# A decoder layer on one core: a shared vector loaded wide, column sums formed in steps, and a tail without filler products

## The chip, the cores and the metric

One Trainium2 chip, one of its cores. The metric is the device time of one execution in microseconds (us), the median of several runs. TensorE, VectorE, ScalarE, GpSimd and SyncE each work through their own list of instructions in order, and wait for each other by semaphores. SyncE issues all loads and stores here. In the profile TensorE is PE (its weight loads are PEld), VectorE DVE, ScalarE ACT, GpSimd POOL, SyncE SP or SPq.

## What is computed

One layer on 256 tokens of 2048 channels, in float32. Cut to what matters:

```
h   = x @ w_in                                  # gMLP u, v; attention q, k, v; two gates
mix = (sigmoid(ga) * (ya @ w_out_a) + sigmoid(gb) * (ob @ w_out_b)) @ w_o
x   = layer_norm(ALPHA * x + mix, ln1_g, ln1_b)
idx, w = route(x, router_w, router_bias)        # top 2 of 16 experts inside one group
ffn = moe(x, idx, w, w_gate, w_up, w_down)      # silu(x Wg) * (x Wu) @ Wd, weighted
ple = sigmoid(x @ ple_w_gate) * (p @ ple_w_proj)
x   = layer_norm(ALPHA * x + ffn + ple, ln2_g, ln2_b)
```

## The kernel before

Nearly all loads are weights: tiles of 128 x 4096 float32, 2 MB each, in the order in which they are used (list `loads`). They go into a pool of twelve large buffers (`B`), where the kernel's long-lived arrays lie too. `done` gives a tile's buffer free once its products are issued, and `prefetch` issues the next load then. SyncE's list is thus: weight, weight, ..., with the small loads where the program asks for them. A load also waits for an earlier load: eight semaphores serve all loads in turn (DMAHW0 to DMAHW7 in the rows of the order).

Short-lived arrays of 128 x 512 come from a pool of five slots (`S`): a new one waits until every reader of the slot's last array has finished.

The first half of the program (projections, attention, output projection) splits each weight piece of 512 columns in two: ScalarE copies it rounded (L267), VectorE takes the difference (L268), three pieces ahead of TensorE, which multiplies both (L286). Four buffers `pc` hold the pieces. Small work that has no place of its own stands in a queue `bg`; one item is taken after every second piece, so a block of 16 pieces takes eight items. The output projection has four blocks (loop `for i in range(4)`), each followed by VectorE's two residual adds (L531) and two statistics (L523). The router's products run on rows that are not normalised yet, and for that the column sums of the router's weights, scaled by ln1_g and ln1_b, are needed: `column_sums` (L513) forms them by two products, two reductions (L516, L517), a product with ones (L519) and a copy (L520), as one item of `bg` in the fourth block.

The expert stage goes over eight pairs of experts (`for g in range(NP)`). For a pair: gate and up products in two halves "A" and "B" (`inner`, L815, eight weight tiles each), then the down products "0" and "1" (`outer`, L822, four tiles each). `evac` (L880, L881) splits the result in yh (ScalarE) and yl (VectorE), `scatter` (L893) puts the rows back by two products, the second of them with yl, and VectorE adds (L898). The scatters of "0" run between the products of "1". A gated embedding `ple` (L793, L798; GpSimd adds it, L805) follows some stages. In the last pair the down products come in narrowing columns (`last_columns`), so that little is left after the last load.

In the pair before the last, ahead of that `evac` of "0", the second norm's vectors are brought in: `gb2` holds ln2_g for columns 0 to 1535 on all partitions, ln2_g and ln2_b for the last 512 columns on all partitions, and in two rows both vectors for columns 0 to 1535. For each vector there is one row load (L1050), one load of 2 KB into a slot `ends` (L1052) and GpSimd's broadcast of it (L1053); a third broadcast (L1054) spreads columns 0 to 1535.

At the end, the last 512 columns are normalised by VectorE alone; for the others a product of two rows (L1095) gives what is added, six times, each followed by VectorE (L1098) and a store. Between these six, `busy(1)` (L547) issues a product of ones with ones.

Of the kernel before, what the change touches and what calls it, by code (L numbers as in the profile page):

```python
# [13 lines left out]
OP = mybir.AluOpType  # L14
AX = mybir.AxisListType
# [4 lines left out]
DC = 16  # L20
NH = 8
NE = 16
# [14 lines left out]
def trunk(ctx, tc, I, out):  # L37
# [19 lines left out]
    def S(name, dt=F32):  # L57
        return tp.tile([128, 512], dt, name=name, tag="t")
# [100 lines left out]
    bg = deque()  # L159
# [350 lines left out]
    lrs = C("lrs", [128, 2])  # L510
    lnm = C("lnm", [128, 2])

    def column_sums():  # L513
        rwb = S("rwb").rearrange("p (c e) -> p c e", c=DC)
        for k, t in ((0, rwg), (1, rwb)):
            DVE.tensor_tensor(t, rw, gc[:, k, :, None].to_broadcast([128, DC, 32]), op=OP.mult)  # L516
            DVE.tensor_reduce(red[:, k], t.rearrange("p c e -> p e c")[:, 0:NE, :], axis=AX.X, op=OP.add)  # L517
        ps = AUX()
        PE.matmul(ps[:, 0:2 * NE], ones, red.rearrange("p k e -> p (k e)"), start=True, stop=True)  # L519
        DVE.tensor_copy(rsb.rearrange("p k e -> p (k e)"), ps[:, 0:2 * NE])  # L520

    def stats(i, a):
        DVE.bn_stats(lst[:, a, i, :], x1[:, a, i * 512:(i + 1) * 512])  # L523

    for i in range(4):
        if i == 3:
            bg.extend([None, column_sums])
        ps = block(mixh, mixl)
        for a in range(2):
            xb = x1[:, a, i * 512:(i + 1) * 512]  # L530
            DVE.scalar_tensor_tensor(xb, xb, ALPHA, ps[a], op0=OP.mult, op1=OP.add)  # L531
            if i < 3:
                stats(i, a)
# [470 lines left out]
    for g in range(NP):  # L1004
        xg, i = xgs[g % 2], g % 2
        following = []
        if g < NP - 1:
            P = Pm[:, 1 - i]
            following.append(lambda P=P, g=g: onehot(P, pair_of(pos, g + 1)))
            if g == 0:  # L1010
                following.extend([lambda P=P, cp=cp: gather(P, xgs[1], cp) for cp in range(8)])
            else:
                following.extend(gathers(P, xgs[1 - i]))
            following.append(lambda P=P, g=g, i=i: selection(P, pair_of(wA, g + 1), 1 - i, g + 1))
        if g == 1:
            bg.extend([None, lambda: keep(2), None, None, None, None])
            bg.extend([lambda q=q, a=a: split_x1(q, a) for q in range(4) for a in range(2)])
        if g > 0:
            bg.extend(following)
        if g == 1:  # L1020
            bg.extend([keep, None, None] + [lambda pr=pr: keep_T(pr) for pr in range(8)] + [free])
        if g == 2:
            bg.extend([lambda q=q, a=a: residual(q, a) for q in range(4) for a in range(2)])
        if g == OVER - 1:
            bg.extend([None] * 20 + [keep])
        if g == NP - 2:
            bg.append(lambda: (free(2), keep()))
        if g == OVER:
            for f in back:
                f()  # L1030
            back = []
            keep(-1)
            overflow()
        ps = inner("A", g, xg, events(back, 1))
        s = hidden(ps, g)
        ples(g, "A")
        ps = inner("B", g, xg, {3: lambda: turn_hidden(s, hTs[0]), **({11: keep} if g == 0 else {})})
        s = hidden(ps, g)
        ples(g, "B")
        if g == 0:  # L1040
            take_late()
            bg.extend(following)
        ps = outer("0", g, {2: lambda: turn_hidden(s, hTs[1]), **({3: keep} if g == 0 else {})})
        if g == 0:
            long["acc"] = BR("acc").rearrange("p (a d) -> p a d", a=2)
        if g == NP - 2:
            gb2 = BR("gb2")
            gbr = gb2[0:2, 2560:4096]
            for k, r in enumerate((I["ln2_g"], I["ln2_b"])):
                SP.dma_start(gb2[k:k + 1, 2560:4096], r[:, 0:1536])  # L1050
                ends = S("ends")
                SP.dma_start(ends[0:1, :], r[:, 1536:2048])  # L1052
                POOL.partition_broadcast(gb2[:, 1536 + 512 * k:2048 + 512 * k], ends[0:1, :], channels=128)  # L1053
            POOL.partition_broadcast(gb2[:, 0:1536], gb2[0:1, 2560:4096], channels=128)  # L1054
        y = evac(ps)
        ples(g, "0")
        at = events(scatters(y, i, 0, g == 0, 0 if g == NP - 1 else None), 1)
        if g == NP - 1:
            last_columns(g, at)
            break  # L1060
        ps = outer("1", g, at)
        drain()
        back = scatters(evac(ps), i, 1024, g == 0)
        ples(g, "1")
# [28 lines left out]
    for n, (q, a) in enumerate((q, a) for q in range(3) for a in range(2)):  # L1093
        ps = MM()
        PE.matmul(ps, rowc[:, a * 128:(a + 1) * 128], gbr[:, q * 512:(q + 1) * 512], start=True, stop=True)  # L1095
        if n < 5:
            busy(1)
        DVE.scalar_tensor_tensor(part(q, a), part(q, a), rstd[:, a:a + 1], ps, op0=OP.mult, op1=OP.add)  # L1098
        store(q, a)

# [63 lines left out]
```

## Time and profile before

| what | value |
|---|---|
| median of three runs | 1624.52 us (1622.77 to 1625.68) |
| the profiled execution | 1626.4 us, its span 1624.7 us |
| mean granted clock of TensorE in it | 0.984 |
| busy: PE, DVE, ACT, POOL | 97%, 34%, 25%, 2% of the span |
| loads and stores | 540.07 MB, 332 GB/s over the span |
| the chain that ended last | PE 26%, DMA 5% of the span |

Busy time counts an instruction from start to modelled end, so a matmul that waits in a full pipeline is busy too. The granted clock is a share of 2.4 GHz; 0.50 is 1.2 GHz. Idle time in brackets stands in front of the instruction, with what ended it. A wait for several things is put down to the one that came last.

### The profile page before, as it was taken

To read this page: it belongs to the slowest core of one execution; us is meant where nothing else is said; L and a number is where in the kernel's file an instruction comes from. 1 tells how busy PE (TensorE), PEld (TensorE's weight loads), DVE (VectorE), ACT (ScalarE), POOL (GpSimd) and SP (SyncE) were. 2 spreads that over 40 slices of the span, in tenths; PEclk is the share of its full clock that TensorE was granted. 3 is DMA by queue.
4 is the path that set the end of the run, shared out by engine and by line. 5 is a ranking of instruction groups with operands and counts; after the bars stand their busy time and mean duration, and the time that the engine had idled before them with its cause. 6 is when DMAs were issued, how large, how long until landed. Compare 5 with 4: busy or idle time off the path is not lost. (4 is left out here: it accounts for less than half of the span.)

```text
span 1624.7 us, 17427 instructions
## 1 busy us (share of the span) xinstructions
PE 1575.2 (97%) x7191; PEld 910.7 (56%) x7191; DVE 548.2 (34%) x948; ACT 407.9 (25%) x717; POOL 37.9 (2%) x43
## 2 busy tenths in 40 slices
PE   8999999999999999999999999999999999985998
PEld 6888878888888875343335353433535353522433
DVE  6555575556556653022222112021011112001105
ACT  5455555454554432011111001001000101000000
POOL 0000000000000000000000000000000000000002
PEclk9999999999999999999999999999999999996998
DMA  9843454354556848999999999998999999999893
GB/s 388 336 156 123 182 201 164 148 184 180 207 186 261 333 159 339 423 426 427 428 427 427 369 426 428 426 427 372 429 426 428 426 428 428 427 428 394 348 428 156
DMA packets 43613, 540.07 MB, mean 332 GB/s; under 512 B 7172, under 2 KB 7172, under 8 KB 10760
## 3 DMA queue, kind: packets, MB, share of 16 engines
q1 hardware_dynamic: 43528, 538.90, 80.8%
q8 instruction: 58, 0.95, 0.2%
q14 instruction: 27, 0.22, 0.0%
HBM read 536.78 MB, written 2.10 MB: 332 GB/s over the span
## 5 line engine op out<-in xcount | busy, mean ns | idle before, releaser
L286 PE MATMUL mm<-pc,xh 128*128 128x512 f32 x1152 | 362.9, 395 | 5.8 <-ACT pc L267 5.2
L268 DVE TENSOR_TENSOR pc<-w,pc 128x512 fp32r<-128x512 f32 x416 | 290.8, 709 | 200.9 <-ACT pc L267 198.2
L267 ACT ACTIVATE pc<-w 128x512 fp32r<-128x512 f32 x416 | 259.6, 630 | 238.0 <-DVE pc L268 179.0
L286 PEld LDWEIGHTS mm<-pc,xh 128*128 128x128 f32 x1152 | 214.0, 189 | 50.9 <-ACT pc L267 5.7
L815 PE MATMUL mm<-w,xg 128*64 128x512 f32 x1024 | 235.3, 604 | 6.1 <-PEq L953 6.1
L822 PE MATMUL mm<-w,hT 128*64 128x512 f32 (+2 forms) x1088 | 236.8, 577 | 3.5 <-DMA w<-in_exp_w_dram 3.5
L815 PE MATMUL mm<-w,late 128*64 128x512 f32 x1024 | 231.0, 597 | 0.0
L286 PE MATMUL mm<-pc,xl 128*128 128x512 f32 x576 | 225.5, 391 | 0.0
L822 PEld LDWEIGHTS mm<-w,hT 128*64 128x64 f32 x1088 | 72.5, 137 | 131.7 <-issue 124.9
L815 PEld LDWEIGHTS mm<-w,xg 128*64 128x64 f32 x1024 | 69.4, 138 | 135.1 <-issue 127.1
L815 PEld LDWEIGHTS mm<-w,late 128*64 128x64 f32 x1024 | 69.0, 136 | 131.0 <-issue 130.4
L286 PEld LDWEIGHTS mm<-pc,xl 128*128 128x128 f32 x576 | 108.5, 188 | 23.1
L798 PE MATMUL mm<-w,x1T 128*128 128x256 f32 x512 | 112.0, 379 | 0.0
L798 PEld LDWEIGHTS mm<-w,x1T 128*128 128x128 f32 x512 | 97.2, 190 | 13.2
L286 PE MATMUL mm<-pc,mixh 128*128 128x512 f32 x256 | 80.2, 394 | 0.0
L859 DVE TENSOR_TENSOR s<-s,mm 128x256 f32<-128x256 f32 x32 | 13.4, 418 | 194.5 <-ACT s L858 194.5
L858 ACT ACTIVATE s<-mm 128x256 f32<-128x256 f32 x32 | 12.3, 383 | 224.3 <-PE mm L815 214.9
L898 DVE TENSOR_TENSOR acc<-acc,aux 128x512 f32<-128x512 f32 (+2 forms) x60 | 38.6, 650 | 87.2 <-PE aux L893 85.3
L880 ACT ACTIVATE yh<-mm 128x512 fp32r<-128x512 f32 (+1 forms) x32 | 18.5, 590 | 185.1 <-PE mm L822 185.1
L881 DVE TENSOR_TENSOR yl<-mm,yh 128x512 fp32r<-128x512 f32 (+1 forms) x32 | 21.6, 682 | 113.2 <-ACT yh L880 78.9
L286 PEld LDWEIGHTS mm<-pc,mixh 128*128 128x128 f32 x256 | 48.6, 191 | 10.1
L286 PE MATMUL mm<-pc,mixl 128*128 128x512 f32 x128 | 50.3, 393 | 0.0
(215 smaller groups left out, 929.4 us busy)
## 6 DMA issues: line engine op xcount, KB each, us to landing
w<-in_exp_w_dram SPq DMA_DIRECT2D x184, 2048.0 KB, 17.9
w<-in_w_in_dram SPq DMA_DIRECT2D x34, 2048.0 KB, 8.7
w<-in_w_o_dram SPq DMA_DIRECT2D x8, 2048.0 KB, 8.3
w<-in_ple_w_gate_dram SPq DMA_DIRECT2D x8, 2048.0 KB, 20.3
w<-in_exp_d_last_dram SPq DMA_DIRECT2D x7, 2048.0 KB, 27.9
w<-in_w_out_a_dram SPq DMA_DIRECT2D x4, 2048.0 KB, 8.2
w<-in_w_out_b_dram SPq DMA_DIRECT2D x4, 2048.0 KB, 8.1
w<-in_w_in_dram SPq DMA_DIRECT2D x3, 1024.0 KB, 10.3
```

Of the source, the lines that this page charges most:

```text
L267: ACT.activation(hi, w, AF.Copy)
L268: DVE.tensor_sub(lo, w, hi.bitcast(F32))
L286: PE.matmul(ps[a], l[:, c, as_], r, start=(first and n == 0), stop=(last and n == 2))
L798: PE.matmul(ps[:, a * 256:(a + 1) * 256], x1T[:, c, a * 128:(a + 1) * 128], w[:, c, :], start=(c == 0 and a == 0), stop=(c == DC - 1), ski ...
L815: PE.matmul(ps[k][es, :], x[:, es], w[:, e, k, :], start=(c == 0), stop=(c == DC - 1), skip_group_check=True, tile_position=(0, 64 * e))
L822: PE.matmul(p[es, 0:n], hTs[fc // 4][:, fc % 4, es], w[:, e, b * n:(b + 1) * n], start=(fc == 0), stop=(fc == 7), skip_group_check=True, t ...
L858: ACT.activation(s[:, ks], pg[:, ks], AF.Sigmoid)
L859: DVE.tensor_mul(s[:, ks], s[:, ks], pg[:, ks])
L880: ACT.activation(h, p[:, 0:n], AF.Copy)
L881: DVE.tensor_sub(l, p[:, 0:n], h.bitcast(F32))
L898: DVE.tensor_add(xb, xb, ps[:, 0:n])
```

## The change

Three edits.

- The last 512 columns of ln2_g and ln2_b are loaded by one load each straight to all 128 partitions of `gb2` (256 KB instead of 2 KB). The slots `ends` and their two broadcasts are gone.
- The column sums are no longer one item of `bg`. From the third block on, each product and each reduction is an item, then come three empty items, then the product with ones and its copy. The slot `rwb` is taken ahead of the loop.
- The products of ones between the six two-row products are gone.

```
+    rwb = S("rwb").rearrange("p (c e) -> p c e", c=DC)
+
     def column_sums():
-        rwb = S("rwb").rearrange("p (c e) -> p c e", c=DC)
-        for k, t in ((0, rwg), (1, rwb)):
-            DVE.tensor_tensor(t, rw, gc[:, k, :, None].to_broadcast([128, DC, 32]), op=OP.mult)
-            DVE.tensor_reduce(red[:, k], t.rearrange("p c e -> p e c")[:, 0:NE, :], axis=AX.X, op=OP.add)
         ps = AUX()
         PE.matmul(ps[:, 0:2 * NE], ones, red.rearrange("p k e -> p (k e)"), start=True, stop=True)
         DVE.tensor_copy(rsb.rearrange("p k e -> p (k e)"), ps[:, 0:2 * NE])
 
+    def sums_bg():
+        for k, t in ((0, rwg), (1, rwb)):
+            bg.append(lambda k=k, t=t: DVE.tensor_tensor(t, rw, gc[:, k, :, None].to_broadcast([128, DC, 32]),
+                                                         op=OP.mult))
+            bg.append(lambda k=k, t=t: DVE.tensor_reduce(red[:, k], t.rearrange("p c e -> p e c")[:, 0:NE, :],
+                                                         axis=AX.X, op=OP.add))
+        bg.extend([None, None, None, column_sums])
...
     for i in range(4):
-        if i == 3:
-            bg.extend([None, column_sums])
+        if i == 2:
+            sums_bg()
         ps = block(mixh, mixl)
...
             for k, r in enumerate((I["ln2_g"], I["ln2_b"])):
                 SP.dma_start(gb2[k:k + 1, 2560:4096], r[:, 0:1536])
-                ends = S("ends")
-                SP.dma_start(ends[0:1, :], r[:, 1536:2048])
-                POOL.partition_broadcast(gb2[:, 1536 + 512 * k:2048 + 512 * k], ends[0:1, :], channels=128)
+                SP.dma_start(gb2[:, 1536 + 512 * k:2048 + 512 * k], r[:, 1536:2048].to_broadcast([128, 512]))
             POOL.partition_broadcast(gb2[:, 0:1536], gb2[0:1, 2560:4096], channels=128)
...
         PE.matmul(ps, rowc[:, a * 128:(a + 1) * 128], gbr[:, q * 512:(q + 1) * 512], start=True, stop=True)
-        if n < 5:
-            busy(1)
         DVE.scalar_tensor_tensor(part(q, a), part(q, a), rstd[:, a:a + 1], ps, op0=OP.mult, op1=OP.add)
```

How instructions stand on the engines, at three places. VectorE in the third and fourth blocks of the output projection, before (L268 is a split, `x16` sixteen in a row, L531 and L523 are residual adds and statistics at a block's end):

```order
L268 TENSOR_TENSOR pc<-w,pc 128x512 x16
L531 SCALAR_TENSOR_TENSOR x_3540<-x_3540,mm 128x512
L523 BN_STATS lst<-x_3540 128x6
L531 SCALAR_TENSOR_TENSOR x_3540<-x_3540,mm 128x512
L523 BN_STATS lst<-x_3540 128x6
L268 TENSOR_TENSOR pc<-w,pc 128x512 x4
L516 TENSOR_TENSOR rwg<-rw,gc 128x512
L517 TENSOR_REDUCE red<-rwg 128x16
L516 TENSOR_TENSOR rwb<-rw,gc 128x512
L517 TENSOR_REDUCE red<-rwb 128x16
L520 COPY rsb<-aux 128x32
L268 TENSOR_TENSOR pc<-w,pc 128x512 x9
```

And now (line numbers of the changed kernel: L537 and L529 are the adds and statistics):

```order
L268 TENSOR_TENSOR pc<-w,pc 128x512 x2
L522 TENSOR_TENSOR rwg<-rw,gc 128x512
L268 TENSOR_TENSOR pc<-w,pc 128x512 x2
L524 TENSOR_REDUCE red<-rwg 128x16
L268 TENSOR_TENSOR pc<-w,pc 128x512 x2
L522 TENSOR_TENSOR rwb<-rw,gc 128x512
L268 TENSOR_TENSOR pc<-w,pc 128x512 x2
L524 TENSOR_REDUCE red<-rwb 128x16
L268 TENSOR_TENSOR pc<-w,pc 128x512 x8
L518 COPY rsb<-aux 128x32
L537 SCALAR_TENSOR_TENSOR x_3540<-x_3540,mm 128x512
L529 BN_STATS lst<-x_3540 128x6
```

The four operations stood in one run between splits of the fourth block; now two splits lie between any two of them, one block earlier, and the copy stands at that block's end.

VectorE at the end of "0" of the pair before the last, with what each instruction waits for, before (L859 and L860 form the hidden values, L870 copies them turned):

```order
L860 SCALAR_TENSOR_TENSOR s<-s,wc,mm 128x256 [waits DVE_49]
L870 COPY hT_4297<-aux 128x256 [waits Activation_49]
L881 TENSOR_TENSOR yl<-mm,yh 128x512 [waits Activation_49]
L881 TENSOR_TENSOR yl<-mm,yh 128x512 [waits DMAHW3_49,Activation_49,Pool_49]
L898 TENSOR_TENSOR acc<-acc,aux 128x512 [waits PE_49] x4
L881 TENSOR_TENSOR yl<-mm,yh 128x512 [waits DVE_49,Activation_49] x2
```

And now:

```order
L866 SCALAR_TENSOR_TENSOR s<-s,wc,mm 128x256 [waits DVE_49]
L876 COPY hT_4297<-aux 128x256 [waits Activation_49]
L887 TENSOR_TENSOR yl<-mm,yh 128x512 [waits Activation_49] x2
L904 TENSOR_TENSOR acc<-acc,aux 128x512 [waits PE_49] x4
L887 TENSOR_TENSOR yl<-mm,yh 128x512 [waits DVE_49,Activation_49]
L887 TENSOR_TENSOR yl<-mm,yh 128x512 [waits DVE_49,Activation_49,Pool_49]
```

The second split of the first two waited for a load and for GpSimd, now for neither; the last split of the next two ("1" of that pair) now names GpSimd.

SyncE around the same place, before (w are weights of the last pair, each behind one of the eight semaphores):

```order
L137 DMA w<-in_exp_w_dram 128x4096 [waits DMAHW1_49,PE_49]
L1050 DMA gb_7941<-in_ln_g_dram 1x1536 [waits DMAHW2_49,PE_49]
L1052 DMA ends<-in_ln_g_dram 1x512 [waits DVE_49,DMAHW3_49,Activation_49,Pool_49]
L1050 DMA gb_7941<-in_ln_b_dram 1x1536 [waits DMAHW4_49]
L1052 DMA ends<-in_ln_b_dram 1x512 [waits DMAHW5_49,DVE_49,Pool_49]
L137 DMA w<-in_exp_w_dram 128x4096 [waits DMAHW6_49,PE_49]
```

And now:

```order
L137 DMA w<-in_exp_w_dram 128x4096 [waits DMAHW1_49,PE_49]
L1056 DMA gb_7941<-in_ln_g_dram 1x1536 [waits DMAHW2_49,PE_49]
L1057 DMA gb_7941<-in_ln_g_dram 128x512 [waits DMAHW3_49]
L1056 DMA gb_7941<-in_ln_b_dram 1x1536 [waits DMAHW4_49]
L1057 DMA gb_7941<-in_ln_b_dram 128x512 [waits DMAHW5_49]
L137 DMA w<-in_exp_w_dram 128x4096 [waits DMAHW6_49,PE_49]
```

Four loads stand in the same four places; two of them are wide and wait for no engine.

## Rows read from the trace of the kernel before

**Rows 1.** The page's span in 40 slices: TensorE and DMA busy, in tenths.
```profile
PE   8999999999999999999999999999999999985998
...
DMA  9843454354556848999999999998999999999893
```

**Rows 2.** Stretches of the tail: us; PE, PEld, DVE, ACT, POOL busy; clock, DMA share, GB/s.
```profile
1440.00:1457.00 17.00, 14.04 (x62) 4.53 (x58) 0.69 (x1) 1.19 (x2) 0.00 (x0) 1.00 1.01 427
1458.00:1482.00 24.00, 0.00 (x0) 0.00 (x0) 0.62 (x2) 0.00 (x0) 1.46 (x3) 0.55 1.01 427
...
1488.00:1512.00 24.00, 24.00 (x112) 16.06 (x108) 2.48 (x4) 1.79 (x3) 1.27 (x1) 1.00 0.61 233
1512.00:1592.00 80.00, 80.00 (x362) 26.54 (x362) 13.94 (x24) 3.47 (x8) 4.51 (x4) 1.00 1.01 428
1592.00:1596.00 4.00, 4.00 (x32) 2.23 (x30) 1.72 (x3) 0.60 (x1) 0.59 (x1) 1.00 0.55 227
```

**Rows 3.** Timeline around TensorE's long wait: start us, us, engine, line, operation [idle before].
```profile
1447.96 3.65 PE L822 MATMUL mm<-w,hT 128*64 128x512 f32 x16 [1.23 <-DMA w<-in_exp_w_dram]
...
1457.70 0.22 SPq L1052 DMA_DIRECT2D ends<-in_ln_g_dram  x1
...
1480.54 1.48 POOL L1053 PARTITION_BROADCAST gb<-ends  x2 [76.13 <-DMA w<-in_exp_w_dram]
1481.38 0.69 DVE L881 TENSOR_TENSOR yl<-mm,yh 128x512 fp32r<-128x512 f32 x1 [34.09 <-POOL gb L1053]
1481.88 1.80 POOL L1054 PARTITION_BROADCAST gb<-gb  x1
...
1482.12 0.80 PE L893 MATMUL aux<-yl,PO 128*128 128x512 f32 x1 [24.46 <-DVE yl L881]
...
1482.85 3.68 PE L822 MATMUL mm<-w,hT 128*64 128x512 f32 x8
...
1494.85 13.98 PE L798 MATMUL mm<-w,x1T 128*128 128x256 f32 x64
```

**Rows 4.** Timeline of VectorE in the output projection's last blocks.
```profile
563.86 0.68 DVE L531 SCALAR_TENSOR_TENSOR x<-x,mm 128x512 f32<-128x512 f32 x1
...
583.65 0.69 DVE L268 TENSOR_TENSOR pc<-w,pc 128x512 fp32r<-128x512 f32 x1 [0.67 <-ACT pc L267]
...
585.62 0.68 DVE L531 SCALAR_TENSOR_TENSOR x<-x,mm 128x512 f32<-128x512 f32 x1
...
591.05 0.69 DVE L516 TENSOR_TENSOR rwg<-rw,gc 128x512 f32<-128x512 f32 x1
591.77 0.58 DVE L517 TENSOR_REDUCE red<-rwg 128x16 f32<-128x256 f32 x1
...
611.41 1.38 DVE L531 SCALAR_TENSOR_TENSOR x<-x,mm 128x512 f32<-128x512 f32 x2 [3.40 <-PE mm L286]
```

**Rows 5.** Timeline of TensorE at the product with ones of the column sums.
```profile
593.71 0.61 PE L519 MATMUL aux<-red,hT 128*128 128x32 f32 x2 [2.61 <-DVE red L517]
594.13 1.20 PE L286 MATMUL mm<-pc,mixh 128*128 128x512 f32 x2
```

**Rows 6.** Timeline of TensorE in the last columns and at the six two-row products (L1095).
```profile
1589.72 4.52 PE L822 MATMUL mm<-w,hT 128*64 128x512 f32 x28
...
1598.73 1.97 PE L822 MATMUL mm<-w,hT 128*64 128x128 f32 x32
...
1607.90 1.12 PE L1095 MATMUL mm<-gb,late 2*128 2x512 f32 x2 [0.46 <-ACT late L1089]
...
1610.64 2.00 PE L1095 MATMUL mm<-gb,late 2*128 2x512 f32 x2
...
1618.20 2.07 PE L1095 MATMUL mm<-gb,late 2*128 2x512 f32 x2
```

**Rows 7.** DMA issues, 150 to 250 us: KB each, us from issue to landing.
```profile
ug<-in_gmlp_ln_b_dram SPq DMA_DIRECT2D x1, 512.0 KB, 7.6
```

**Rows 8.** A stretch among the two-row products, columns as in rows 2.
```profile
1612.00:1616.00 4.00, 4.00 (x6) 1.05 (x6) 1.50 (x2) 0.00 (x0) 0.00 (x0) 0.50 0.34 131
```

## The prediction

> **What bounds the kernel now.** I read the page's slices first, then the tail by stretches, then the instructions around the one long hole in TensorE, then the two smaller places that the change touches.
>
> In the slices TensorE is busy at 0.9 nearly throughout and the DMA engines are full in most slices of the second half [rows 1]. So in the expert stage two resources are near their limits at once, and what a hole costs depends on which one is ahead. The stretches of the tail say it [rows 2]. From 1440 to 1457 us the DMA engines move 427 GB/s and TensorE is busy 14.04 of 17 us: weights are late. The reader sees it at single tiles: the products of a weight tile start 1.23 us after TensorE had nothing left, when the load lands, and take 3.65 us [rows 3]. From 1458 to 1482 TensorE does nothing at all, the loads go on at 427 GB/s, and the granted clock drops (0.55, that is mostly 1.2 GHz). From 1488 to 1512 the picture is turned: TensorE is busy 24 of 24 us and the loads fall to 233 GB/s, because the buffers that filled in the hole are not free. From 1512 to 1592 both are full, and the loads end between 1592 and 1596.
>
> The hole itself [rows 3]: TensorE starts the second product of a scatter at 1482.12, after 24.46 us of waiting for VectorE's split yl. VectorE waits 34.09 us for GpSimd's broadcast out of "ends". GpSimd waits for the four small loads; SyncE issues the first of "ends" at 1457.70, behind weights already asked for, and the broadcasts start at 1480.54. So yl stands only because its slot in the five-slot pool was lent to "ends".
>
> **Edit 1: the wide load.** It removes "ends", thus the wait (the order rows of the split show it without the GpSimd and DMA waits), and two broadcasts of about 0.74 us each on GpSimd, which lie on no path once yl is free. What is late next? Not TensorE's own work but the weights, as before 1457. TensorE alone would gain 24.46 us and some 3 us of slow clock (eight products took 3.68 us at 1482.85 instead of 1.9 at full clock [rows 3]). The weights allow less: the bytes of the tail stay, and only the time in which the loads ran below rate can come back. That is the stretch of 24 us at 233 GB/s against 428: 24 x (1 - 233/428) = **10.9 us**. For this the buffers must never fill. The longest product group that holds them is the 14 us of L798 [rows 3], in which 14/4.9 = 3 tiles arrive (4.9 us a tile: 2 MB at 428 GB/s); in the 24 us of the hole five tiles arrived and the loads had not slowed yet, so there is room.
>
> The wide loads add bytes: 256 KB each. At the stream's 428 GB/s each takes 0.6 us. A bound from above is the 512 KB broadcast of the first norm's vectors, two together landing 7.6 us after issue [rows 7], so at most 3.8 us for our two; a load that stands first in a full queue does not pay the issue latency, so I take 0.6 us each, 1.2 us in all, ends 1.2 and 3.8. All four loads now stand before the next weight tile in SyncE's queue as the four small ones did, with the same lane waits; GpSimd's remaining broadcast (1.8 us) and the gated-embedding add behind it wait until they land, near 1482, and the add's input comes only after L798 of that pair, near 1485 (the end of its row in rows 3 less the hole), so nobody waits.
>
> Last, TensorE trailed the loads at the end: the third-last tile's products began near 1592.3 (12 of the 28 in the row at 1589.72 belong to the tile before) [rows 6], some 1.2 us after its load can have landed (1596 less 4.9 for the 2 MB behind it). On the heels of the loads it trails by some 0.3 us: **1 us** more, bounds 0 and 4 (the last tile's products begin halfway through the row at 1598.73, near 1599.7, the loads end by 1596). After that the chain is TensorE's own and unchanged. Edit 1: 10.9 - 1.2 + 1.0 = 10.7 us, bounds 7.1 and 13.7.
>
> **Edit 2: column sums in steps.** Blocks of the output projection are 21.76 us apart (563.86 to 585.62, first residual add to first residual add); the one that holds the sums takes 25.79 us (to 611.41) [rows 4]: 4.03 us more. The reason is in the rows: four VectorE operations in one go from 591.05 on (0.69 and 0.58 us, twice), while TensorE waits 2.61 us for the reduction, and the products after it run at half clock (two took 1.20 us) [rows 5]. Now each of the four stands alone between two pairs of splits. VectorE's cycle there is 0.69 us busy and 0.67 idle [rows 4]; a pair of pieces has 1.34 us idle, an added operation takes 0.69 or 0.58. So they hide. At the head of that block VectorE is still paying the two adds and two statistics of the block before (0.68 us each); the first added operation comes two splits later. If that cover is gone, TensorE stands up to 0.69 us per operation and the gain goes. The product with ones moves to the block's end, where its input is long ready; it keeps 0.2 us of TensorE (0.4 at half clock [rows 5]). The copy of its result waits for it with VectorE's residual adds queued behind, and those wait for the same last products. Gain 4.03 - 0.2 = 3.8 us, bounds 0 and 4.0. TensorE is the only busy resource from there to 1093 us and the loads are paced by the buffers it frees, so I carry it in full; 0 is the other bound.
>
> **Edit 3: no ones between two-row products.** From 1607.90 to 1620.27 six two-row products and five of ones run in a row, 12.4 us [rows 6]. The ones did not hold the clock: in the stretch from 1612 TensorE is busy 4.00 of 4 us at 0.50 [rows 8]. The first product starts at 1607.90, follows to the next in 1.05 us at full clock, and the third runs slow already (the clock falls about 2.8 us in). If it falls there again, 2.7 products go at 1.05 and 3.3 at 2.0: 9.5 us, gain **2.9**. If it falls at once: 12.0, gain 0.4; if never: 6.3, gain 6.1. I take 2.9, since the fall came with the ones in place. VectorE's add (0.75 us) and the stores hide behind the next product.
>
> By the Trainium skill (TensorE: Matmul & The Clock Gate, Part 1) a busy engine is held at 2.4 GHz and an idle one at 1.2; by that alone all six would stay fast and edit 3 would give 6.1. The row at 0.50 with TensorE fully busy speaks against it for two-row products.
>
> **Sum.** 10.7 + 3.8 + 2.9 = 17.4 us. The profiled execution took 1626.4 us (span 1624.7), so 1609.0 in its place; it stands 1.9 above the median of the runs, 1624.5, and on that scale I forecast **1607.1 us**.
>
> **The rivals.**
> *Column sums give nothing at the end* (10%): VectorE falls behind as said, or the weights absorb it. For: the loads bind before 1457. Against: below rate at 1488 and before, they follow TensorE's frees. Time 1624.5 - 13.6 = 1610.9.
> *The clock holds in the last six* (6%): gain 6.1 instead of 2.9, 1603.9. Against: rows 8.
> *Edit 1 does not do what it says* (5%): another reader holds yl's slot, or the second pair of splits inherits the GpSimd wait that the order rows show there. For: that wait is printed. Against: GpSimd's only other reader of that pool is the embedding add of long before. Then 1624.5 - 6.7 = 1617.8.
> *Slower* (3%): with the hole gone TensorE waits for weights at every tile to the end, and its clock could fall there. At half clock a tile takes 7.3 us (twice 3.65; eight took 3.68 [rows 3]) against 4.9 for its load, 2.4 us each; of some 24 tiles left it is slower by over 0.2% from 20.6/2.4, nine, on; with twelve, 1636. Against: from 1440 to 1457, with just such waits, the granted clock is 1.00 [rows 2].
> The same page (section on HAM oscillation) reports a thin-product kernel that fell back to the slow clock at every weight tile it waited for; by that all tiles would be slow, and the case would be the likeliest. The stretch at 1.00 disagrees, so I leave it at 3%.
>
> **How the numbers follow.** The forecast has 76%, the rivals 10, 6, 5 and 3. A measurement of this kernel tells about 0.2%, 3.2 us, from no change. All but the last case are faster by more; of its 3% one part ends within. Faster 0.97, same 0.01, slower 0.02. The range: downwards the clock case and 4 us of lag, 1602.5; upwards the column case with dear wide loads, 1612.5. It leaves out the stall that stays, the slower case and the tails of the first.
>
> **What would show it.** Right: no wait of yl on GpSimd and no standing of TensorE over 3 us after 1400; loads above 420 GB/s until they end, near 1582 (1595 less 9.7 less 3.8); TensorE waiting about 1.2 us at weight tiles at clock 1.00 in the last 80 us; blocks of the projection all near 21.8 to 22.0 us; the six two-row products in 9 to 10 us. Wrong: loads that still fall below rate after 1480, a projection block above 23 us, or a clock of 0.50 before the last columns.

## The result, and the profile after

The changed kernel takes 1607.47 us (median of four runs, 1606.60 to 1610.06); the kernel before, on the same chip, 1625.10 (1622.77 to 1626.67). The ratio is 0.9895, with a 95% interval of 0.9878 to 0.9912: 17.6 us less. The forecast was 1607.1 in a range of 1602.5 to 1612.5. The profiled execution took 1607.34 us, its span 1605.6, so 19.1 us less span than before.

The slices of the page, to be held against [rows 1], with the rate of the loads:

```profile
PE   8999999999999999999999999998999999999978
...
DMA  9843453445556858999999999999999999999995
GB/s 388 345 158 112 182 204 146 183 158 209 176 191 262 326 201 319 418 427 427 428 426 428 365 428 427 427 426 377 429 427 427 427 427 427 427 429 422 428 427 204
```

The slices with 8 and 5 near the end of TensorE's line are gone, and so is the dip in the loads behind them. The same stretches as in [rows 2], and the end of the loads (us; busy times; clock, DMA share, GB/s):

```profile
1440.00:1457.00 17.00, 15.28 (x64) 4.68 (x60) 4.14 (x6) 1.19 (x2) 0.00 (x0) 1.00 1.00 426
1458.00:1482.00 24.00, 21.99 (x94) 16.08 (x92) 2.07 (x3) 1.79 (x3) 1.80 (x1) 0.93 1.00 420
1482.00:1512.00 30.00, 30.00 (x135) 9.74 (x133) 3.73 (x7) 0.77 (x2) 1.26 (x1) 1.00 1.01 428
1512.00:1570.00 58.00, 46.07 (x207) 14.63 (x204) 4.68 (x10) 2.70 (x6) 0.00 (x0) 1.00 1.01 427
...
1578.00:1580.00 2.00, 2.00 (x19) 1.03 (x15) 0.69 (x1) 0.60 (x1) 0.40 (x1) 1.00 0.62 254
1580.00:1582.00 2.00, 2.00 (x14) 1.28 (x14) 1.23 (x2) 0.00 (x0) 0.00 (x0) 1.00 0.35 147
1582.00:1584.00 2.00, 2.00 (x27) 1.53 (x24) 1.86 (x4) 0.38 (x1) 1.73 (x2) 1.00 0.00 0
```

In the tail the loads no longer fall to 233 GB/s before they end; they are over at 1582, where before they still ran at 227 from 1592 to 1596 [rows 2]. What bounds the tail now can be read in the fourth row: TensorE stands 12 us in the 58 up to 1570, at a clock of 1.00. It waits for weights. Timeline of TensorE (start us, us, engine, line, operation, idle before):

```profile
1442.67 3.65 PE L828 MATMUL mm<-w,hT 128*64 128x512 f32 x16 [1.24 <-DMA w<-in_exp_w_dram]
...
1462.96 3.02 PE L799 MATMUL aux<-late 128*128 128x256 f32 x8 [2.01 <-DMA late<-in_ple_w_proj_dram]
...
1567.97 1.94 PE L828 MATMUL mm<-w,hT 128*64 128x512 f32 x8 [1.24 <-DMA w<-in_exp_d_last_dram]
...
1575.52 4.52 PE L828 MATMUL mm<-w,hT 128*64 128x512 f32 x28
```

Where the hole of 24.46 us stood [rows 3], the longest wait is 2.01 us, for a small load of the gated embedding, which the hole had covered. The 28 products of the last columns start 14.20 us earlier than in [rows 6]. VectorE's split yl (line 887 now) waits no more for GpSimd. The view of that tile gives the instruction (ns shortest/median/longest), and what VectorE waited for ahead of it (us, times):

```profile
L887 DVE TENSOR_TENSOR yl<-mm,yh x32: 425/692/693, 709.5 to 1583.5; 128x512 fp32r<-128x512 f32 x31, 128x256 fp32r<-128x256 f32 x1
its engine sat idle before it (us, times) until:
  ACT yh L886: 81.7, 26
  DVE yl L887: 0.4, 1
```

VectorE in the projection's last two blocks, to be held against [rows 4]:

```profile
563.64 0.68 DVE L537 SCALAR_TENSOR_TENSOR x<-x,mm 128x512 f32<-128x512 f32 x1
...
567.47 0.69 DVE L522 TENSOR_TENSOR rwg<-rw,gc 128x512 f32<-128x512 f32 x1
569.28 0.62 DVE L524 TENSOR_REDUCE red<-rwg 128x16 f32<-128x256 f32 x1
...
585.74 0.68 DVE L537 SCALAR_TENSOR_TENSOR x<-x,mm 128x512 f32<-128x512 f32 x1
...
606.83 1.38 DVE L537 SCALAR_TENSOR_TENSOR x<-x,mm 128x512 f32<-128x512 f32 x2 [3.40 <-PE mm L286]
```

The block with the four operations takes 22.10 us and the last one 21.09, where before it was 21.76 and 25.79. Last, the six two-row products, one row now, VectorE's last adds, which wait for them, and the stretches in which they run:

```profile
1593.70 7.53 PE L1099 MATMUL mm<-gb,late 2*128 2x512 f32 x12 [0.46 <-ACT late L1093]
...
1599.56 0.75 DVE L1100 SCALAR_TENSOR_TENSOR acc<-acc,frs,mm 128x512 f32<-128x512 f32 x1 [0.96 <-PE mm L1099]
1601.27 0.75 DVE L1100 SCALAR_TENSOR_TENSOR acc<-acc,frs,mm 128x512 f32<-128x512 f32 x1 [0.96 <-PE mm L1099]
```

```profile
1594.00:1596.00 2.00, 2.00 (x6) 0.79 (x5) 1.03 (x2) 0.00 (x0) 0.00 (x0) 1.00 0.64 228
1596.00:1597.00 1.00, 1.00 (x4) 0.51 (x3) 0.89 (x2) 0.00 (x0) 0.00 (x0) 0.92 0.53 207
1597.00:1601.00 4.00, 4.00 (x5) 1.09 (x4) 1.81 (x3) 0.00 (x0) 0.00 (x0) 0.50 0.62 210
```

The six products take 7.53 us, 12.37 before [rows 6]; the clock falls just before 1597 and stays at 0.50 with TensorE busy all the time, as in [rows 8].

So the 19.1 us of the two traces split at three places. Up to the fourth block's residual adds it is 4.6 us (611.41 and 606.83; 0.2 of it lay there before the third block). From there to the row of 28 products it is 9.6 (978.31 and 968.69 us long), and in the last six products 4.8.

### The profile page after: what moved, and what is told of

The parts are those of the page before. It is cut to its first block, busy times and chain, and to the rows that moved or that the text cites. A ratio compares the mean times of both kernels' runs of the same rounds, so it can differ in the third digit from the quotient of the medians.

```text
span 1605.6 us, 17410 instructions
## 1 busy us (share of the span) xinstructions
PE 1568.4 (98%) x7186; PEld 909.0 (57%) x7186; DVE 548.5 (34%) x948; ACT 408.0 (25%) x717; POOL 36.6 (2%) x41
## 5 line engine op out<-in xcount | busy, mean ns | idle before, releaser
L268 DVE TENSOR_TENSOR pc<-w,pc 128x512 fp32r<-128x512 f32 x416 | 290.9, 710 | 197.2 <-ACT pc L267 194.4
```

The source lines that it names most:

```text
L268: DVE.tensor_sub(lo, w, hi.bitcast(F32))
```

## The experiments

The kernels of one set ran on the same chip and share the runs of the kernel before; there are three sets, named in the headings. Three lengths are read off each trace and shown together further down: the third and fourth projection blocks, the way from there to the 28 products, and the last six products.

### Each edit alone (first set)

**Edit 1 alone.** On the kernel before:

```
-                ends = S("ends")
-                SP.dma_start(ends[0:1, :], r[:, 1536:2048])
-                POOL.partition_broadcast(gb2[:, 1536 + 512 * k:2048 + 512 * k], ends[0:1, :], channels=128)
+                SP.dma_start(gb2[:, 1536 + 512 * k:2048 + 512 * k], r[:, 1536:2048].to_broadcast([128, 512]))
```

> The kernel before with edit 1 alone. Theory (the slot lent to `ends` held yl, and behind it only weights are late): no wait of yl on GpSimd, no standing of TensorE over 3 us after 1400 us, loads at some 428 GB/s to their end. The prediction's sum gives 10.7 us less than before (7.1 to 13.7); what the changed kernel's trace leaves when about 4.4 us is taken for edit 2 (two projection blocks 4.36 us shorter) is 14.2 - 4.4 = 9.8 us less. Rival 1, TensorE's own time set the end: the whole hole comes back, 24 us or more less. Rival 2, edit 1 works only together with edit 2: 2 us less or nothing.

Measured: 1617.37 us against 1625.11, ratio 0.9950 (0.9937 to 0.9964): 7.7 us less, interval 5.9 to 10.2. In the trace the way from the projection to the 28 products is 968.79 us, 9.5 less than before. VectorE's yl waits for ScalarE and for itself only (81.9 and 0.4 us in all), TensorE's longest wait after 1400 us is 2.0 us, and the loads run at 424 to 428 GB/s in the stretches from 1458 to 1570. So the tail's gain is edit 1's and needs no help from edit 2, and both rivals fall: 24 us do not come back, and neither is it nothing. The median lies below the 9.8 that the theory gave, inside the interval.

**Edit 2 alone.** On the kernel before, the first two pieces of the change's diff: the operations as items of `bg` from the third block on.

> The kernel before with edit 2 alone. Theory (a block of the projection some 4 us shorter, TensorE the only busy resource there, so all of it is carried to the end): 3.8 to 4.4 us less than before. Rival, weights absorb it, since the hole at 1458 us waits for loads and stays where it is: 0 to 1 us less, with the hole longer by what the blocks gain.

Measured: 1622.01 us, ratio 0.9980 (0.9971 to 0.9989): 3.1 us less, interval 1.8 to 4.7. The hole is still there, and as long as it was but for 0.2 us ([rows 3] has 24.46):

```profile
1477.90 0.79 PE L899 MATMUL aux<-yl,PO 128*128 128x512 f32 x1 [24.68 <-DVE yl L887]
```

It moved 4.2 us to the front (from 1482.12). The weights did not absorb the gain.

**Edit 3 alone.** On the kernel before:

```
         PE.matmul(ps, rowc[:, a * 128:(a + 1) * 128], gbr[:, q * 512:(q + 1) * 512], start=True, stop=True)
-        if n < 5:
-            busy(1)
```

> The kernel before with edit 3 alone. Theory after the changed kernel's trace (two-row products in a row take 0.86 us each at full clock and 1.71 at half, and not the 1.05 and 2.0 that stood between products of ones): 4.8 us less than before. The prediction's own pricing: 2.9 us less. If the clock falls at once: 0.4 less; if it never falls: 6.1 less.

Measured: 1621.92 us, ratio 0.9981 (0.9971 to 0.9991): 3.2 us less, interval 1.5 to 4.7. The trace gives more, 7.50 us where there were 12.37:

```profile
1607.28 7.50 PE L1095 MATMUL mm<-gb,late 2*128 2x512 f32 x12 [0.46 <-ACT late L1089]
```

Of the four prices written down this trace fits 4.8, while the median lies nearest to 2.9; its interval shuts out 0.4 and 6.1, and 4.8 lies just outside it. The three medians add up to 14.0 us, the whole change has 17.6. With intervals of 3 to 4 us each that is no contradiction, and the lengths in the traces add up.

**The slot alone.** On the kernel before: the narrow load and the broadcast stay, but in the vector's own place.

```
-                ends = S("ends")
-                SP.dma_start(ends[0:1, :], r[:, 1536:2048])
-                POOL.partition_broadcast(gb2[:, 1536 + 512 * k:2048 + 512 * k], ends[0:1, :], channels=128)
+                own = gb2[0:1, 1536 + 512 * k:2048 + 512 * k]
+                SP.dma_start(own, r[:, 1536:2048])
+                POOL.partition_broadcast(gb2[:, 1536 + 512 * k:2048 + 512 * k], own, channels=128)
```

> The kernel before, with the 2 KB load put into row 0 of its final place and GpSimd's broadcast done in place: no slot is lent, but the narrow load and both broadcasts stay. Theory (the lent slot alone made the hole; the wide load is only another way to do without it, and costs its bytes): 10.7 + 1.2 = 11.9 us less than before, so 0.5 to 3.8 us less than the run with the wide load. Rival, GpSimd's broadcasts or their wait for the small loads cost time in themselves: the hole or a part of it stays, at most 5 us less than before.

Measured: 1615.21 us, ratio 0.9932 (0.9918 to 0.9947): 9.9 us less, interval 8.6 to 13.3, and 2.2 less than with the wide load. GpSimd waits as long as ever for the small loads and broadcasts as late as before ([rows 3]: 1480.54), and nobody stands for it:

```profile
1480.53 1.48 POOL L1053 PARTITION_BROADCAST gb<-gb  x2 [76.01 <-DMA gb<-in_ln_b_dram]
1481.87 1.80 POOL L1054 PARTITION_BROADCAST gb<-gb  x1
```

So it was the lent slot and not the broadcast that made the hole. The wide load looks like the dearer way to do without the slot, by 2.2 us at the medians, whose ranges do not overlap (1616.25 to 1617.56 and 1612.42 to 1615.55).

### What the wide load costs (second and third set)

**Each wide load twice.** On the changed kernel:

```
+                for _ in range(2):
-                SP.dma_start(gb2[:, 1536 + 512 * k:2048 + 512 * k], r[:, 1536:2048].to_broadcast([128, 512]))
+                    SP.dma_start(gb2[:, 1536 + 512 * k:2048 + 512 * k], r[:, 1536:2048].to_broadcast([128, 512]))
```

> The changed kernel with each wide load issued twice, so 0.52 MB more. The run with the narrow load in its own row was about 2.1 us faster than the one with the wide load, where the prediction had priced the two wide loads at 1.2. Theory (a wide load costs more than its bytes at the stream's rate): 2 us or a little more over the changed kernel, about 1609.6 us. Rival, bytes alone: 1.2 us more, 1608.7. Rival, hidden: 1607.5, and the 2.1 us then come from elsewhere.

Measured: 1617.77 us, 10 more than the changed kernel's 1607.47: none of the three. The way to the 28 products, 978.64 us, is as long as it was with the hole. The experiment measured something else. The second load writes where the first one does and so waits for its landing, and SyncE stands with all the weights behind it. Its timeline (the time of a row reaches from the first issue to the last), and the stretches there:

```profile
1453.07 26.12 SPq L1058 DMA_DIRECT2D gb<-in_ln_g_dram  x2
1479.24 0.28 SPq L1056 DMA_DIRECT2D gb<-in_ln_b_dram  x1
1479.58 4.70 SPq L1058 DMA_DIRECT2D gb<-in_ln_b_dram  x2
1484.38 15.60 SPq L137 DMA_DIRECT2D w<-in_exp_w_dram  x10
```

```profile
1453.00:1479.00 26.00, 23.73 (x99) 15.58 (x98) 2.76 (x4) 1.19 (x2) 1.80 (x1) 0.93 0.89 375
1479.00:1485.00 6.00, 6.00 (x28) 2.88 (x26) 0.69 (x1) 0.60 (x1) 0.20 (x1) 1.00 0.44 90
```

From 1453 to 1484 us no weight is asked for, and the DMA engines run dry (share 0.44 at the end of it). Against 428 GB/s the two stretches lose 3.2 and 4.7 us of load time; the bytes of 0.52 MB are 1.2 us. So most of the 10 us is the price of a load that waits for a landing in the queue that all weights share.

**Two wide loads more, into other columns.** On the changed kernel; GpSimd's last broadcast writes over them.

```
                 SP.dma_start(gb2[:, 1536 + 512 * k:2048 + 512 * k], r[:, 1536:2048].to_broadcast([128, 512]))
+                SP.dma_start(gb2[:, 512 * k:512 + 512 * k], r[:, 1536:2048].to_broadcast([128, 512]))
```

> The changed kernel with two wide loads more (256 KB each), into columns that GpSimd's last broadcast writes over afterwards, so that no load waits for another's landing, as it did in the run with each load issued twice. Theory (about 1 us a wide load): 2 us more than the changed kernel. Rival, bytes at the stream's rate: 1.2 us more. Rival, hidden: no difference. If it is 5 us or more, it is not the bytes but the places that small loads take in SyncE's queue in front of the weights.

**The changed kernel again**, in the same set:

> The changed kernel once more, on the chip of this set, to have the differences of the three others against it. All theories: 1607.5 us, within 1.5; the six last products between 6 and 9 us, since they took 7.5 in the changed kernel, 6.1 and 9.1 in two experiments that leave them alone.

**All three edits with the narrow load in its own row**, in the same set (the edit is that of the slot alone, on the changed kernel):

> All three edits, but with the narrow load into the row of its final place and GpSimd's broadcast in place of the wide load. Theory (the two wide loads cost the tail about 2.1 us, and the lent slot alone made the hole): some 2 us less than the changed kernel, 1605.4 us. Rival, the wide loads cost their bytes alone: 1.2 us less, 1606.3. Rival, no difference: 1607.5, and the 2.1 us between the two runs on the kernel before were something else.

Measured on one chip: narrow 1607.23 us (1605.83 to 1608.36, ratio 0.9890, 0.9875 to 0.9905), two wide 1609.65 (1608.85 to 1610.50, ratio 0.9902, 0.9887 to 0.9917), four wide 1613.50 (1611.79 to 1615.86, ratio 0.9928, 0.9915 to 0.9942). At the medians the first two wide loads cost 2.4 us, the next two 3.9. The changed kernel misses what was expected of it here, 1607.5 within 1.5, by 0.7, and its six last products took 9.18 us instead of 6 to 9; so the narrow kernel is held against 1609.65 and not against 1607.5.

The medians also hold the scatter of the last six products (9.18 us in this trace, 7.74 in the narrow one). The way to the 28 products is free of it: 967.07 us narrow, 969.80 with two wide loads, 973.69 with four. Over all traces (table below) the first pair costs 2.1 us and the next 4.6, and no trace with two wide loads comes nearer than 1.3 us to one without. That is more than their bytes, 1.2 us a pair at the stream's rate, and not hidden; the theory's 2 us fits the first pair and is about half of what the second costs. In the run with four, while they pass (clock, DMA share, GB/s):

```profile
1476.00:1480.00 4.00, 4.00 (x20) 3.37 (x18) 0.00 (x0) 0.00 (x0) 0.00 (x0) 1.00 0.97 312
1480.00:1484.00 4.00, 4.00 (x18) 1.33 (x18) 0.69 (x1) 0.60 (x1) 0.00 (x0) 1.00 0.95 290
```

The DMA engines are busy 0.97 and 0.95 of the time, nearly as at 428 GB/s, and move 312 and 290. So in this stretch it is not an empty queue, as the expectation had it for a large cost: the engines are busy longer for the bytes that they move. A wide load moves 2 KB a partition, a weight tile 16 KB, and all 128 partitions of a wide load read the same row of memory; which of the two matters was not tried. The lost rate in these 8 us (2.4 us of load time) and the bytes of all four loads (2.4 us) make 4.8 of the 6.8 us by which this trace exceeds the narrow ones. The rest was not found.

### Who sets the tail's end (second set)

On the changed kernel, in `inner`:

```
                 if j:
                     done()
+                    if g == NP - 1:
+                        busy(2)
```

> The changed kernel with two products of ones (0.23 us each) behind each of the sixteen gate and up tiles of the last pair: 7.4 us of work more on TensorE, which changes no result. Theory (weights set the end: eleven waits of TensorE for tiles between 1518 and 1570, some 12 us in all, take it up): the same time as the changed kernel, 1607.5, with shorter waits and the loads ending where they ended; at most 1 us more. Rival, TensorE's own work sets the end: 7 us more, 1615.

Measured: 1608.49 us, ratio 0.9888 (0.9873 to 0.9903). The second set has no run of the changed kernel; that has 1607.47 in the result above and 1609.65 in the third set, so no difference can be told. TensorE's waits for weights from 1480 to 1575 us (us in total, times, longest), in the changed kernel and then with the added products, whose stretch from 1518 to 1548 stands below:

```profile
PE mm L821 <- DMA w<-in_exp_w_dram: 6.4, 6, 1.2
PE mm L828 <- DMA w<-in_exp_d_last_dram: 5.6, 5, 1.3
```

```profile
PE mm L828 <- DMA w<-in_exp_d_last_dram: 3.1, 3, 1.2
1518.00:1548.00 30.00, 30.00 (x136) 8.96 (x136) 1.56 (x4) 0.52 (x2) 0.00 (x0) 1.00 1.01 428
```

The waits shrink from 12.0 us to 3.1: 8.9 us, near what the sixteen pairs of added products take (0.54 us from their start to the next start for most of them, some 8 in all). TensorE runs behind the loads meanwhile, has no wait from 1518 to 1548, and waits for the last tiles again. The loads keep their 428 GB/s, and the way to the 28 products is 969.90 us, where kernels without the added work have 968.36 to 969.80. So the weights set the end.

### What made the fourth block long (second set)

On the changed kernel, the four operations in one item of `bg` (in the third block), the product with ones where the change put it:

```
+        def four():
+            for k, t in ((0, rwg), (1, rwb)):
+                DVE.tensor_tensor(t, rw, gc[:, k, :, None].to_broadcast([128, DC, 32]), op=OP.mult)
+                DVE.tensor_reduce(red[:, k], t.rearrange("p c e -> p e c")[:, 0:NE, :], axis=AX.X, op=OP.add)
+        bg.extend([None, four, None, None])
         bg.extend([None, None, None, column_sums])
```

> The changed kernel with the four operations of the column sums in one run again, but in the third block, and their product with ones at that block's end as in the changed kernel. Theory (what cost time was TensorE standing in its own order at the product with ones, 2.61 us, and the slow clock behind it; the splits run three pieces ahead, 4 us, and four operations in a run take 2.5): within 1 us of the changed kernel, projection blocks of 22 to 23 us. Rival (the run of four puts the splits behind TensorE): a block of 24 us or more, 2 to 4 us more than the changed kernel, 1610 to 1611.5.

Measured: 1608.79 us, ratio 0.9889 (0.9874 to 0.9904). That is 1.3 more than the changed kernel's 1607.47, where within 1 was expected. Its last six products took 9.06 us instead of 7.53, so it is the block that decides. VectorE there:

```profile
563.87 0.68 DVE L537 SCALAR_TENSOR_TENSOR x<-x,mm 128x512 f32<-128x512 f32 x1
...
569.31 0.69 DVE L523 TENSOR_TENSOR rwg<-rw,gc 128x512 f32<-128x512 f32 x1
570.03 0.63 DVE L524 TENSOR_REDUCE red<-rwg 128x16 f32<-128x256 f32 x1
570.57 0.69 DVE L523 TENSOR_TENSOR rwb<-rw,gc 128x512 f32<-128x512 f32 x1
571.29 0.62 DVE L524 TENSOR_REDUCE red<-rwb 128x16 f32<-128x256 f32 x1
...
585.96 0.68 DVE L537 SCALAR_TENSOR_TENSOR x<-x,mm 128x512 f32<-128x512 f32 x1
```

The block takes 22.09 us with the four in one go, and they begin 5.4 us after the block's first residual add, as they did in the kernel before (591.05 and 585.62 [rows 4]). VectorE has room for them either way. What cost 4 us was the product with ones right behind the reduction: TensorE stood 2.61 us at it [rows 5] and came back at half clock. The stretch behind it in the kernel before (the first figure after the busy times is the clock):

```profile
594.00:597.00 3.00, 3.00 (x9) 2.42 (x9) 0.79 (x2) 0.00 (x0) 0.00 (x0) 0.50 0.39 82
```

### The last six products over 128 rows (second and third set)

On the changed kernel: both operands of the last products on all 128 partitions, 126 of them zero.

```
-        long["rowc"] = t[0:2, 3584:3840]
+        long["rowc"] = t[:, 3584:3840]
+        DVE.memset(long["rowc"], 0.0)
...
-            gbr = gb2[0:2, 2560:4096]
+            gbr = gb2[:, 2560:4096]
+            POOL.memset(gbr, 0.0)
...
-    ACT.activation(rowc, ps[0:2, 0:T], AF.Copy)
+    ACT.activation(rowc[0:2, :], ps[0:2, 0:T], AF.Copy)
```

> The changed kernel with the six last products taken over all 128 rows instead of two, the other 126 rows zero: the same result, the same columns and passes. Theory (the clock fell with TensorE busy all the time, so it is the two rows): the clock stays 1.00 to the last product, six products take 6 x 0.86 = 5.2 us instead of 7.5, 2.3 us less than the changed kernel, 1605.2. Rival (the clock falls there whatever the rows): no difference, 1607.5, or slightly more for setting the rows to zero ahead of the loads.

Measured: 1605.92 us, ratio 0.9876 (0.9861 to 0.9892), near the theory's 1605.2; the rival's 1607.5 is above all runs. The trace settles it: the six products take 5.39 us, the clock is 1.00 from 1592 to 1601. And the same with the narrow load in its own row, third set:

> The run before this one with the last six products over 128 rows (126 of them zero). Theory (the two savings lie in different places, the loads' end and TensorE's clock behind it, and add): 2 us less than the run with 128 rows and the wide loads, 1603.8 us; the clock 1.00 to the last product and VectorE's six adds back to back. Rival, they do not add: 1605.5 or more.

Measured: 1604.90 us (1604.29 to 1605.04), ratio 0.9875 (0.9859 to 0.9890). The forecast was 1603.8 and the rival 1605.5 or more, both counted from another chip, and the median lies between. On its own chip the changed kernel has 1609.65 with no run below 1608.85: 4.7 us or 0.3% more. In the trace both savings are there, the way of 967.02 us and the six products in 5.39, so they add. This version beats both kernels. Its last products on TensorE, and the stretch in which they run:

```profile
1592.76 5.39 PE L1103 MATMUL mm<-gb,late 128*128 128x512 f32 x12 [0.56 <-ACT late L1097]
```

```profile
1594.00:1598.00 4.00, 4.00 (x10) 1.52 (x8) 3.56 (x5) 0.00 (x0) 0.00 (x0) 1.00 0.60 212
```

The same columns and passes, at a clock of 1.00 to the end, and behind them VectorE's adds without a gap:

```profile
1593.89 5.04 DVE L1104 SCALAR_TENSOR_TENSOR acc<-acc,frs,mm 128x512 f32<-128x512 f32 x6 [1.35 <-PE mm L1103]
```

### Three lengths in all the traces

| what is in the kernel | us, in each trace | mean |
|---|---|---|
| third and fourth block, sums as one item | 47.55 (before), 47.60, 46.05, 47.65 | 47.2 |
| the same with sums in steps or in the third block | 43.19 or 43.20, ten traces | 43.2 |
| fourth block's adds to the 28 products, with the hole | 978.31 (before), 977.75, 978.89 | 978.3 |
| the same, two wide loads | 968.69 (after), 968.79, 969.90, 968.81, 968.36, 969.80 | 969.1 |
| the same, narrow loads in their own row | 966.71, 967.07, 967.02 | 966.9 |
| the same, four wide loads | 973.69 | |
| the same, each of two wide loads twice | 978.64 | |
| six last products with ones between | 12.37 (before), 12.27, 12.61, 12.63 | 12.5 |
| the same without ones | 7.53 (after), 7.50, 6.11, 6.85, 9.06, 7.74, 7.36, 9.18 | 7.7 |
| the same over 128 rows | 5.39, 5.39 | 5.4 |

The first three steps of the change are thus 4.0, 9.2 and 4.8 us. The last line but one scatters most, by 3 us: it depends on where the clock falls.

## Why the prediction was right

**The bound.** Right in each part that was tried. Weights are late before the hole and, with the hole gone, up to 1568. The slot lent to "ends" caused the hole, as the run with the slot alone shows. The run with more work on TensorE shows that weights set the end.

**Edit 1: 10.7 forecast (7.1 to 13.7), 9.2 in the traces, 7.7 (5.9 to 10.2) alone.** The main term was right: regained load time 10.9 and TensorE's lag 1.0 make 11.9, and with narrow loads, which add no bytes, the traces give 978.3 - 966.9 = 11.4. The loads themselves show the 10.9. They end within the half microsecond from 1595.5 before, from 1585.0 and 1580.5 in two narrow runs; counted from the fourth block's adds (611.41, 611.89, 607.08) that is 11.0 and 10.7 us earlier. So the lag gave some 0.5 instead of 1.0. Its working has the third-last tile start near 1592.3; twelve of the 28 products at that row's own pace (4.52 us for 28) end at 1591.7, which would have made it 0.3. The term that was mis-sized is the price of the wide loads, "0.6 us each, 1.2 us in all": the traces give 969.1 - 966.9 = 2.1 us (rounded from the single lengths), the medians 2.2 and 2.4. The price came from bytes at the stream's rate; the bound from above, 3.8 [rows 7], held it.

**Edit 2: 3.8 forecast (0 to 4.0), 4.0 in the traces, 3.1 (1.8 to 4.7) alone.** The size was right and it was carried to the end in full. The reason for carrying it was not quite right: from 660 us on TensorE is not "the only busy resource". In the kernel before (columns as in [rows 2]) the DMA engines are full there too:

```profile
680.00:880.00 200.00, 200.00 (x926) 73.31 (x922) 47.34 (x96) 31.15 (x65) 0.00 (x0) 1.00 1.01 427
```

That the loads follow the buffers which TensorE frees does fit: SyncE waits for TensorE's gate and up products 60 times, 256.3 us in all, from 560 to 1100. Of the reason for the long block half was right. The sentence that named it put "four VectorE operations in one go" beside TensorE's wait; the run with the four in one go and the product late shows that only the wait and the slow clock behind it cost anything. To spread the four out was not needed.

**Edit 3: 2.9 forecast (0.4 to 6.1), 4.8 in the traces, 3.2 (1.5 to 4.7) alone.** The mechanism was right: the clock falls with the ones gone as it fell with them. The mis-sized step is "2.7 products go at 1.05 and 3.3 at 2.0". Those were times from one product to the next product of ones, as two rows of the kernel before show behind those at 1607.90 and 1610.64 [rows 6], 1.05 and 1.94 us after them:

```profile
1608.95 0.39 PE L547 MATMUL aux<-ones_b 128*128 128x512 bf16 x1
...
1612.58 0.61 PE L547 MATMUL aux<-ones_b 128*128 128x512 bf16 x1
```

In a row of their own kind, VectorE's last adds follow each other in 1.71 us (0.75 and a wait of 0.96) at half clock, so 0.86 at full. With the fall 2.8 us in, as forecast, that is 3.3 products at 0.86 and 2.7 at 1.71, 7.5 us, which is what this trace has. That it fits so well is chance in part: the same row took 6.11 to 9.18 us in eight traces, so the place of the fall is no constant. What the products next to one of ones pay for beyond that was not tried.

**The sum.** 17.4 forecast; 4.0, 9.2 and 4.8 are 18.0 in the traces, 17.6 at the medians. Edit 1's error (1.5 too much) and edit 3's (1.9 too little) went against each other, and in the third set the same kernel took 1609.65: the closeness of 1607.1 to 1607.47 is partly luck. The ends of the range do not follow from the words beside them: the clock case with 4 us of lag would be 1603.9 - 3.0 = 1600.9, the column case with dear wide loads 1610.9 + 2.6 = 1613.5. The measured time lies inside either way.

**The rivals.** *Column sums give nothing at the end* fell: edit 2 alone moves the end. *The clock holds in the last six* fell for two rows (0.50 from 1597 on); over 128 rows, which the prediction did not consider, the clock held. By the Trainium skill (TensorE: Matmul & The Clock Gate, Part 1) a busy engine runs at 2.4 GHz. The traces agree for 128 rows, and for two rows they do not, with TensorE busy 4.00 of 4 us at 0.50. *Edit 1 doesn't do what it says* fell: yl does not wait for GpSimd; the wait that the order showed on the last split of the pair is never the last to end. *Slower* fell: TensorE waits 1.24 us at tile after tile up to 1568, and the clock is 1.00 from 1482 to 1594. The section on HAM oscillation on the same page of the Trainium skill reports slow restarts for a kernel in which the products of a tile took less time than the wait for the next. Here a tile's products take 3.65 us and the wait 1.24, so the prediction's "by that all tiles would be slow" read more into the section than it says, and the 3% did not need the stretch at 1.00 against it.

**The signs.** Of those named, the wait of yl, the end of the loads at 1582 (forecast: near 1582) and the tiles at 1.00 in the last stretch came out as written. The loads' rate was 420 in one stretch and 426 to 428 in the others up to 1570, where above 420 was forecast. The blocks were 22.10 and 21.09 (21.8 to 22.0 forecast), and the six products took 7.5 instead of 9 to 10. One sign of being wrong showed for a moment: the clock fell ahead of the last columns, behind the wait of 2.01 us.

```profile
1464.00:1468.00 4.00, 4.00 (x13) 3.16 (x12) 0.00 (x0) 0.00 (x0) 0.00 (x0) 0.61 1.02 426
```

It did not last: from 1468 to 1472 the clock is 1.00 again.

One thing is open: alone, each edit's median gains 0.9 to 1.6 us less than its traces, inside the interval for edits 1 and 2 and just outside it for edit 3. The kernel before ranges from 1621.5 to 1627.5 in 21 runs of that set.

## What to carry to other kernels

Where a small load shares a pool with work in the middle of a stage, the work inherits the place of that load in the queue; give the load a place of its own first, and only then ask whether it must be wide. What a hole costs at the end of a stage that is bound by loads is not its length but the load time lost while the buffers were full: stretch times (1 - low rate / full rate), here 10.9 us for a hole of 24.46, with 11.4 measured. A price for an operation in a row of its own kind must not be read off rows where another kind stands in between.

## What was not expected of the hardware

- In the two-row products the clock fell to 0.50 while TensorE was busy all the time; the same products over 128 rows, 126 of them zero, ran at 1.00 to the end in two traces (5.39 us instead of 6.1 to 9.2). The point of the fall shifts from run to run of like code.
- Wide loads of 2 KB a partition took the stream from 428 to 290 GB/s at a DMA share of 0.95: about 1.1 us for 256 KB in the first pair, where bytes alone are 0.6, and 2 or more for each of a second pair (3.9 to 4.6 us for the two, from one trace).
- A wait of 2.01 us of TensorE for a small load at 1462.96 was followed by eight products in 3.02 us. The same wait (1.99 to 2.02 us) was followed by 1.97 us at a clock of 1.00 in six traces, that of the sums in one item among them, and by 2.42 to 3.38 us in four others. The slow clock cost the end nothing: the way to the 28 products is 968.69 us with it, and 968.36, 968.81 and 969.80 in traces with two wide loads and without it.
